# 32 bytes of room behind each k-tile of the weights' high and low parts in a decoder layer

## The chip, the cores and the metric

The kernel runs on one core of a Trainium2 chip. The metric is the device time of one execution in microseconds (us); of the kernel before, three runs have a median of 1816.47 us (1816.28 to 1816.69). Everything is float32 in memory. The tensor engine (PE) takes two operands from the on-chip memory (SBUF, 128 partitions): the stationary one, which a separate instruction (LDWEIGHTS, row PEld) puts into the array, and the moving one, which is streamed past it, one column after the other.

## The reference

One decoder layer, 256 positions wide 2048: a modulation vector from `c` (`w_ada`), a normed input, one large projection, three token mixers side by side, their projections, gates and an output projection, then a gated MLP with a short convolution. Cut to the products with large weights, where the kernel spends its time:

```python
mod = silu(c) @ w_ada + b_ada                      # 2048 x 12288
h = rmsnorm(x, g_mix) * (1 + sc1) + sh1
z = h @ w_in                                       # 2048 x 16392
merged = sig(gm) * (out_m @ w_branch[0]) + sig(gd) * (out_d @ w_branch[1]) + sig(gs) * (out_s @ w_branch[2])
x = x + gt1 * (merged @ w_out)                     # 2048 x 2048
hid = (rmsnorm(x, g_ffn) * (1 + sc2) + sh2) @ w_up # 2048 x 11264
x = x + gt2 * ((silu(conv(hid[:, :5632])) * hid[:, 5632:]) @ w_down)
```

## The kernel before

Each product with a weight matrix runs through `gemm` (line 332). It walks over k-tiles (128 rows of the weight matrix), four at a time. `weights` (line 312) loads four k-tiles by 512 columns (1 MB, line 319) into a tile `raw`, and for each pair of k-tiles makes two tiles of 128 x 2 x 512: `hi`, a rounded copy in the engine's reduced float32 form (ScalarE, ACT, line 324), and `lo`, what the rounding left over (VectorE, DVE, line 326). The activations are kept in a high and a low part as well (`hh` and `hl`, and so on). A product is the sum of three: high by high, high weights by low activations, low weights by high activations.

`mms` (line 346) has three forms, which are told apart by their lines in the profile:

- "F" (line 371): the weights are stationary, 128 columns at a time; 256 columns of activations move. `hi` meets the high and the low activations, `lo` the high ones.
- "T" (line 369): the activations are stationary; the weights move, 512 columns (440 in one part of the input projection).
- "H" (line 355, the up projection): the weights are stationary; with `hi`, the high and low activations of one k-tile move in one matmul of 512 columns, with `lo` the high ones, 256 columns.

Every matmul has its own weight load, for the stationary operand changes each time. In "F" with 512 weight columns and 16 k-tiles, a call issues 16 x 4 x 3 = 192 matmuls; a branch projection (8 k-tiles) issues 96.

Where the operands lie follows from the order of the tile pools and the sizes of their tiles. The pools are laid out one after the other: `const` (small constants, among them `ones_r` and `tri`), `slots` (the activations), `rawp`, `adap`, `hip` (four `hi` buffers), `lop` (four `lo` buffers), `tmp`. In `slots` the slot of tag `s2` is laid out first and has (2 x 4 x 257 + 8) x 4 = 8256 bytes in each partition (line 64), 64 more than a multiple of 512; every other slot has 8192 or 16384, `raw` has 8192, `acc` 2048, `ada` 4096, and `hi` and `lo` have 2 x 512 x 4 = 4096. So in the built program each of the eight weight buffers, each k-tile in it and each activation tile begins at 480 bytes past a multiple of 512; a step of 128 columns is 512 bytes. One GEMM operand is not there: `oml` (line 787), the low part of the first branch's activations, lies in the slot `s2` and begins 64 bytes earlier, at 416. The constants `ones_r` and `tri` begin at 128 past a multiple of 512.

`tri_f` (line 96) is a 128 x 128 mask that is written by GpSimd (line 91) and read once, by the copy to `tri` on line 98. `small` (line 76) is a group of three rotating buffers of 1 KB.

Order: a scheduler sets the order of the instructions on each engine when the program is built; DMA loads are issued by SyncE in the order of the text, tied to one another by `issue_after`.

Of the kernel before, what the change touches and what calls it, by code (L numbers as in the profile page):

```python
# [10 lines left out]
F32 = mybir.dt.float32  # L11
F32R = mybir.dt.float32r
# [5 lines left out]
P = 128  # L18
# [10 lines left out]
EPS = 1e-6  # L29
LAM_INIT = 0.8 - 0.6 * math.exp(-0.3 * 0)  # L30
BIG = 3.0e38

C_MQ, C_MK, C_MV, C_MO = 0, 1024, 2048, 3072
C_IF = 4096
# [5 lines left out]
def kernel(  # L40
# [11 lines left out]
    const = ctx.enter_context(tc.tile_pool(name="const", bufs=1))  # L52
# [3 lines left out]
    hip = ctx.enter_context(tc.tile_pool(name="hip", bufs=4))  # L56
    lop = ctx.enter_context(tc.tile_pool(name="lop", bufs=4))
# [18 lines left out]
    def small(name):  # L76
        return tmp.tile([P, 256], F32, tag="small", name=name, bufs=3)
# [9 lines left out]
    A.copy(ones_r, ones)  # L87

    def masked(name, base, fill, chan, step, cmp):
        m = const.tile([P, P], F32, name=name)  # L90
        nc.gpsimd.memset(m, base)
        nc.gpsimd.affine_select(out=m, in_=m, compare_op=cmp, fill=fill, base=0,
                                pattern=[[step, P]], channel_multiplier=chan)
        return m

    tri_f = masked("tri_f", 1.0, 0.0, 1, -1, ALU.is_gt)
    tri = const.tile([P, P], F32R, name="tri")
    A.copy(tri, tri_f)
    mstrict = masked("mstrict", 1.0, 0.0, -1, 1, ALU.is_gt)
    mcausal = masked("mcausal", 1.0, 0.0, -1, 1, ALU.is_ge)  # L100
    mdiff = masked("mdiff", BIG, -BIG, 1, -1, ALU.is_ge)
    eps_c = const.tile([P, 1], F32, name="eps_c")
# [209 lines left out]
    def weights(rows, nk, n, hold=None):  # L312
        if nk == 2:
            raw = adap.tile([P, 2, 512], F32, tag="ada", name="raw2")
        else:
            raw = rawp.tile([P, 4, 512], F32, tag="raw", name="raw")
        with tc.issue_after(state["load"].ins) if not state["started"] else nullcontext():
            state["started"] = True
            state["load"] = nc.sync.dma_start(raw[:, :nk, :n], rows.rearrange("(k p) f -> p k f", p=P))
        his, los = [], []  # L320
        for k0 in range(0, nk, 2):
            hi = hip.tile([P, 2, 512], F32R, tag="hi", name="hi")
            lo = lop.tile([P, 2, 512], F32R, tag="lo", name="lo")
            A.copy(hi[:, :, :n], raw[:, k0:k0 + 2, :n])  # L324
            with tc.issue_after(hold.ins) if hold else nullcontext():
                state["split"] = V.tensor_tensor(lo[:, :, :n], raw[:, k0:k0 + 2, :n], hi[:, :, :n].bitcast(F32),  # L326
                                                 ALU.subtract)
            his.append(hi)
            los.append(lo)
        return his, los  # L330

    def gemm(orient, act, W, row0, col0, n, kt0, kt1, hold=None, hold_all=False, acc=None):
# [40 lines left out]
        for s0 in range(kt0, kt1, 4):  # L373
            nk = min(4, kt1 - s0)
            r0 = row0 + s0 * P
            wh, wl = weights(W[r0:r0 + nk * P, col0:col0 + n], nk, n, hold if s0 > kt0 or hold_all else None)
            last = s0 + nk >= kt1
            for ks in ([range(nk)] if last else [range(k0, k0 + 2) for k0 in range(0, nk, 2)]):
                for t in range(nt):
                    mms(t, ks, s0, wh, wl)  # L380
            if not last:
                tick()
# [561 lines left out]
    for k in range(0, KD, 2):  # L944
# [3 lines left out]
        for j in range(2):  # L948
            b = b2[:, k + j:k + j + 1]
            hi, lo = h2act(k + j)[:, 0:S], h2act(k + j)[:, S:2 * S]  # L950
# [85 lines left out]
```

## Time and profile before

| | |
|---|---|
| median of three runs | 1816.47 us |
| profiled execution, its own time | 1817.8 us |
| its span, first to last instruction | 1816.1 us |
| mean granted share of PE's clock | 0.994 |
| PE busy / weight loads busy | 1774.3 / 1605.4 us |
| DVE busy / ACT busy | 1333.4 / 907.1 us |
| matmuls | 11045 |

A matmul's duration in the profile is longer than the distance to the next one, since they overlap; a row that says "PE gp L371 x432" in the chain of waits gives a stretch in which nothing but such matmuls follow one another, and its length by its count is the spacing. In operand names, `gp<-hh,hi` is the output tile, then the two inputs; the lines tell which of them moves.

### The profile page before, as it was taken

To read this page: it belongs to the slowest core of one execution; us is meant where nothing else is said; L and a number is where in the kernel's file an instruction comes from. 1 tells how busy PE (TensorE), PEld (TensorE's weight loads), DVE (VectorE), ACT (ScalarE), POOL (GpSimd) and SP (SyncE) were. 2 spreads that over 40 slices of the span, in tenths; PEclk is the share of its full clock that TensorE was granted. 3 is DMA by queue.
4 is the path that set the end of the run, shared out by engine and by line. 5 is a ranking of instruction groups with operands and counts; after the bars stand their busy time and mean duration, and the time that the engine had idled before them with its cause. 6 is when DMAs were issued, how large, how long until landed. Compare 5 with 4: busy or idle time off the path is not lost.

```text
span 1816.1 us, 27533 instructions
## 1 busy us (share of the span) xinstructions
PE 1774.3 (98%) x11045; PEld 1605.4 (88%) x11045; DVE 1333.4 (73%) x1787; ACT 907.1 (50%) x1221; POOL 9.5 (1%) x30
## 2 busy tenths in 40 slices
PE   4989999999999999999999999999999999999998
PEld 4888999999988999999999878888888888888887
DVE  5998867887888687686897568888875556666654
ACT  5533345666565554543444465555553335555532
POOL 0000000000000000000000000000000000000000
PEclk9989999999999999999999999999999999999999
DMA  9988965766778467677898547777765555555563
GB/s 300 338 299 295 315 199 165 262 233 212 240 251 276 163 218 257 219 239 268 286 316 279 184 152 248 254 263 273 263 207 191 197 192 186 188 189 192 196 209 116
DMA packets 219644, 423.55 MB, mean 233 GB/s; under 512 B 8768, under 2 KB 31613, under 8 KB 219005
## 3 DMA queue, kind: packets, MB, share of 16 engines
q1 hardware_dynamic: 217693, 417.56, 68.5%
q0 software_dynamic: 544, 2.11, 0.3%
q8 instruction: 86, 1.41, 0.3%
q10 hardware_dynamic: 1280, 2.14, 0.3%
q14 instruction: 41, 0.34, 0.1%
HBM read 419.68 MB, written 2.10 MB: 232 GB/s over the span
## 4 chain that ended last, share of the span: by engine, by line
PE 91%; DVE 3%; DMA 3%; ACT 1%; issue 1%; SPq 0%; DVEq 0%; ACTq 0%
PE gp L369 30%; PE gp L371 29%; PE acch L355 27%; PE kept L371 2%; DMA raw<-in_w_in_dram 2%; DMA raw<-in_w_ada_dram 1%; DVE lo L326 1%; DVE quads L212 1%; PE psc L627 0%; ACT hi L324 0%; PE pm L228 0%; PE pr L303 0%; DVE acc L212 0%; PE px L935 0%; PE ptf L685 0%
## 5 line engine op out<-in xcount | busy, mean ns | idle before, releaser
L326 DVE TENSOR_TENSOR lo<-raw,hi 128x1024 fp32r<-128x1024 f32 (+1 forms) x608 | 728.1, 1207 | 364.4 <-ACT hi L324 338.1
L324 ACT CAST hi<-raw 128x1024 fp32r<-128x1024 f32 (+1 forms) x608 | 622.7, 1038 | 706.5 <-PE gp L369 225.5
L355 PE MATMUL acch<-h,hi 128*128 128x512 f32 x1408 | 427.9, 395 | 1.8 <-DVE h L952 1.8
L371 PE MATMUL gp<-hh,hi 128*128 128x256 f32 x1152 | 299.8, 285 | 2.3 <-ACT skT L499 2.2
L355 PEld LDWEIGHTS acch<-h,lo 128*128 128x128 f32 x1408 | 252.5, 188 | 54.1
L371 PE MATMUL gp<-hl,hi 128*128 128x256 f32 x1152 | 298.3, 283 | 0.0
L355 PE MATMUL acch<-h,lo 128*128 128x256 f32 x1408 | 263.7, 279 | 0.0
L355 PEld LDWEIGHTS acch<-h,hi 128*128 128x128 f32 x1408 | 221.6, 189 | 10.6 <-DVE h L952 2.0
L371 PEld LDWEIGHTS gp<-hh,hi 128*128 128x128 f32 x1152 | 220.9, 192 | 4.0 <-ACT skT L499 2.4
L371 PEld LDWEIGHTS gp<-hl,hi 128*128 128x128 f32 x1152 | 220.9, 192 | 0.2
L371 PE MATMUL gp<-hh,lo 128*128 128x256 f32 x1152 | 218.3, 284 | 0.5 <-DVE lo L326 0.5
L212 DVE SCALAR_TENSOR_TENSOR acc<-araw,ccol,acc 128x512 f32<-128x512 f32 x240 | 178.8, 745 | 4.0 <-DMA araw<-in_w_ada_dram 2.1
L371 PEld LDWEIGHTS gp<-hh,lo 128*128 128x128 f32 x1152 | 173.2, 192 | 1.1 <-DVE lo L326 0.7
L369 PE MATMUL gp<-hi,hh 128*128 128x440 f32 (+1 forms) x416 | 159.9, 384 | 3.6 <-DVE sv L501 1.4
L369 PE MATMUL gp<-hi,hl 128*128 128x440 f32 (+1 forms) x416 | 158.1, 380 | 0.0
L369 PE MATMUL gp<-hi,ath 128*128 128x512 f32 x352 | 137.0, 389 | 0.0
L369 PE MATMUL gp<-hi,atl 128*128 128x512 f32 x352 | 136.9, 389 | 0.0
L369 PE MATMUL gp<-lo,hh 128*128 128x440 f32 (+1 forms) x416 | 112.9, 378 | 2.3 <-DVE lo L326 2.3
L369 PE MATMUL gp<-lo,ath 128*128 128x512 f32 x352 | 105.8, 389 | 0.0
L369 PEld LDWEIGHTS gp<-hi,hh 128*128 128x128 f32 x416 | 79.3, 191 | 15.8 <-PE gp L369 2.4
L369 PEld LDWEIGHTS gp<-lo,hh 128*128 128x128 f32 x416 | 78.0, 189 | 13.7 <-DVE lo L326 3.6
L369 PEld LDWEIGHTS gp<-hi,hl 128*128 128x128 f32 x416 | 79.3, 191 | 10.4 <-issue 0.7
(346 smaller groups left out, 2059.9 us busy)
## 6 DMA issues: line engine op xcount, KB each, us to landing
raw<-in_w_in_dram SPq DMA_DIRECT2D x98, 1024.0 KB, 5.0
raw<-in_w_up_dram SPq DMA_DIRECT2D x88, 1024.0 KB, 5.1
araw<-in_w_ada_dram SPq DMA_DIRECT2D x128, 512.0 KB, 5.4
raw<-in_w_down_dram SPq DMA_DIRECT2D x44, 1024.0 KB, 5.1
raw<-in_w_ada_dram SPq DMA_DIRECT2D x62, 512.0 KB, 5.2
raw<-in_w_branch_dram SPq DMA_DIRECT2D x24, 1024.0 KB, 5.3
raw<-in_w_in_dram SPq DMA_DIRECT2D x21, 880.0 KB, 4.7
raw<-in_w_out_dram SPq DMA_DIRECT2D x16, 1024.0 KB, 5.2
```

Source lines behind the costliest of these rows:

```text
L212: V.scalar_tensor_tensor(acc, raw[:, k, :], ccol[:, kt:kt + 1], acc, ALU.mult, ALU.add)
L324: A.copy(hi[:, :, :n], raw[:, k0:k0 + 2, :n])
L326: state["split"] = V.tensor_tensor(lo[:, :, :n], raw[:, k0:k0 + 2, :n], hi[:, :, :n].bitcast(F32), ALU.subtract)
L355: T.matmul(acc[t][:, 0:m], lhsT=w[k // 2][:, k % 2, sl], rhs=ah(s0 + k)[:, 0:m], start=start, stop=s0 + k == kt1 - 1 and w is wl, skip_gro ...
L369: T.matmul(o, lhsT=a(s0 + k)[:, sl], rhs=wk[:, :n], **kw)
L371: T.matmul(o, lhsT=wk[:, sl], rhs=a(s0 + k), **kw)
```

## The change

Each `hi` and `lo` tile becomes 128 x 2 x 520, of which the first 512 columns of each k-tile are used. A buffer has 4160 bytes instead of 4096, and the second k-tile in it begins 2080 bytes after the first instead of 2048. The sixteen k-tiles of the eight buffers begin at 0, 32, 64, ..., 480 bytes past the place of the activations, counted modulo 512, each of these once. The copy and the subtraction that fill a buffer with 512 columns now work on two pieces of 512 elements in a partition instead of one of 1024 (the ones with 440 columns were in two pieces before). To make room, `tri_f` is no longer a tile of its own but takes one of the rotating `small` buffers. All tiles from the slots to `adap` lie 512 bytes lower. No instruction is added, taken out or moved: on each engine the same operations stand in the same order.

```diff
+SKEW = 8
...
     def masked(name, base, fill, chan, step, cmp):
-        m = const.tile([P, P], F32, name=name)
+        m = small("tri_f")[:, 0:P] if name == "tri_f" else const.tile([P, P], F32, name=name)
...
-            hi = hip.tile([P, 2, 512], F32R, tag="hi", name="hi")
-            lo = lop.tile([P, 2, 512], F32R, tag="lo", name="lo")
+            hi = hip.tile([P, 2, 512 + SKEW], F32R, tag="hi", name="hi")
+            lo = lop.tile([P, 2, 512 + SKEW], F32R, tag="lo", name="lo")
```

## Rows read from the trace of the kernel before

**Rows 1.** page, part 1: busy us (share of the span) xinstructions

```profile
PE 1774.3 (98%) x11045; PEld 1605.4 (88%) x11045; DVE 1333.4 (73%) x1787; ACT 907.1 (50%) x1221; POOL 9.5 (1%) x30
```

**Rows 2.** page, part 4: the chain that ended last, shares of the span

```profile
PE 91%; DVE 3%; DMA 3%; ACT 1%; issue 1%; SPq 0%; DVEq 0%; ACTq 0%
```

**Rows 3.** chain of waits in order of time: start us, us, what

```profile
291.99 14.40 PE gp L369 x72
...
785.63 51.84 PE gp L371 x432
...
913.30 34.35 PE gp L371 x288
...
948.12 34.35 PE gp L371 x288
...
1185.34 55.84 PE acch L355 x320
...
1349.35 129.88 PE gp L369 x573
```

**Rows 4.** PE groups by form, xcount | busy us, mean ns of one | idle

```profile
L355 PE MATMUL acch<-h,hi 128*128 128x512 f32 x1408 | 427.9, 395 | 1.8 <-DVE h L952 1.8
...
L371 PE MATMUL gp<-hh,hi 128*128 128x256 f32 x1152 | 299.8, 285 | 2.3 <-ACT skT L499 2.2
...
L369 PE MATMUL gp<-hi,ath 128*128 128x512 f32 x352 | 137.0, 389 | 0.0
...
L369 PE MATMUL gp<-hi,hh 128*128 128x440 f32 x224 | 83.9, 375 | 2.8 <-DVE sv L501 1.1 <-DVE dk L501 1.0 <-DVE dv L501 0.7
...
L369 PE MATMUL gp<-hi,hh 128*128 128x512 f32 x192 | 76.0, 396 | 0.8 <-ACT skT L499 0.5 <-DVE sv L501 0.3
```

**Rows 5.** instructions of one tile, GEMM lines: duration ns min/median/max

```profile
L371 PE MATMUL gp<-oml,hi x128: 277/279/286, 866.7 to 981.7; 128*128 128x256 f32 x128
...
L371 PE MATMUL gp<-odh,hi x128: 280/283/468, 715.7 to 842.8; 128*128 128x256 f32 x128
...
L369 PE MATMUL gp<-hi,atl x352: 389/389/397, 1348.5 to 1810.1; 128*128 128x512 f32 x176
...
L355 PE MATMUL acch<-h,hi x1408: 387/396/497, 1078.5 to 1701.7; 128*128 128x512 f32 x176
...
L355 PE MATMUL acch<-h,lo x1408: 274/278/285, 1079.8 to 1702.3; 128*128 128x256 f32 x176
```

**Rows 6.** instructions of four lines with a constant as stationary: duration ns min/median/max

```profile
L303 PE MATMUL pr<-parts,ones_r x16: 393/395/398, 883.6 to 1349.0; 128*128 128x512 f32 x16
...
L567 PE MATMUL puA<-hlB,ones_r x4: 282/290/297, 309.3 to 388.2; 128*128 128x256 f32 x4
...
L568 PE MATMUL puA<-hlB,ones_r x4: 281/282/286, 309.4 to 388.3; 128*128 128x256 f32 x4
...
L565 PE MATMUL puB<-hlB,tri x4: 278/281/281, 306.5 to 385.8; 128*128 128x256 f32 x4
```

**Rows 7.** DVE and ACT groups by form of the split, same columns as rows 4

```profile
L326 DVE TENSOR_TENSOR lo<-raw,hi 128x1024 fp32r<-128x1024 f32 x552 | 669.0, 1221 | 349.9 <-ACT hi L324 327.8 <-PE gp L369 17.0 <-PE pdt L612 1.7
...
L326 DVE TENSOR_TENSOR lo<-raw,hi 128x880 fp32r<-128x880 f32 x56 | 59.2, 1068 | 14.5 <-ACT hi L324 10.3 <-PE gp L369 3.2 <-ACT ht L432 0.8
...
L324 ACT CAST hi<-raw 128x1024 fp32r<-128x1024 f32 x552 | 572.0, 1050 | 636.4 <-PE gp L369 201.4 <-PE gp L371 173.8 <-PE acch L355 157.8
...
L324 ACT CAST hi<-raw 128x880 fp32r<-128x880 f32 x56 | 50.7, 926 | 70.1 <-DMA raw<-in_w_in_dram 41.0 <-PE gp L369 24.0 <-DVE ez L570 4.0
```

**Rows 8.** PE waits for the low part: us in total, times, longest us

```profile
PE gp L369 <- DVE lo L326: 2.3, 2, 1.3
...
PE gp L371 <- DVE lo L326: 0.5, 1, 0.5
```

**Rows 9.** lines 98 and 429: duration ns min/median/max, first and last start us

```profile
L98 ACT CAST tri<-tri_f x1: 292/292/292, 2.8 to 2.8; 128x128 fp32r<-128x128 f32 x1
...
L429 DVE TENSOR_SCALAR ht<-xnT,a,b x2: 408/410/411, 28.6 to 29.0; 128x256 f32<-128x256 f32 x2
```

## Prediction

> **What bounds the kernel now.** I read the page's busy shares first. The tensor engine is busy 98% of the span with 11045 matmuls, VectorE 73%, ScalarE 50% [rows 1]. The chain that ended last gives PE 91% and VectorE 3% [rows 2], so the question is what one matmul costs. The chain in order of time has long stretches of nothing but matmuls of one form; length by count is their spacing [rows 3]: 51.84 us by 432 is 120.0 ns for form F (256 columns), 129.88 by 573 is 226.7 ns for T with 512 columns, 14.40 by 72 is 200.0 ns for T with 440, 55.84 by 320 is 174.5 ns as the mean of H, which alternates 512 and 256 columns. A spacing of exactly 120.0 ns over 432 matmuls while loads, copies and subtractions go on beside them says that it is made inside the engine and not by a neighbour.
>
> Two stretches of F differ. The rows at 913.30 and 948.12 hold 288 matmuls each, 192 of the gate and 96 of the first branch, in 34.35 us. With 192 at 120.0 ns (23.04 us) the 96 are left 11.31 us, or 117.8 ns. Shape, order and engine are the same; what differs is that one in three of the 96 moves `oml`, the only GEMM operand that does not begin at 480 bytes modulo 512 but 64 lower. The durations say it too: 279 ns median for `oml`, 283 for `odh` [rows 5]. So the place of one operand against the other does change the spacing. Durations exceed spacings by a constant 162 to 163 ns (283 against 120.0, 389 against 226.7), so a row of durations can be read as a row of spacings.
>
> The Trainium skill (TensorE: Matmul & The Clock Gate, Step-by-step: what each phase is for) says that the weight load and the moving operand have independent read ports and that loading the next weights takes no bandwidth from the running matmul. The 117.8 against 120.0 ns do not fit it, if the place is the cause; by the rule alone the change would be worth 0 us.
>
> **The change part by part.** Nothing is added or moved on any engine, so the terms are differences of spacing times counts.
>
> F: 128 x 3 groups for `kept`, 1152 x 3 for `hh`/`hl` (one of them in [rows 4]) and 128 x 9 for the three branches make 4992 matmuls; 384 of them, those of the first branch, already have the mixed distance, which leaves 4608. In the changed kernel the stationary buffers lie at sixteen distances from the activations. The nearest row is the 117.8 ns, a gain of 2.2 ns; but there one operand in three is shifted, by one fixed amount. The few other matmuls whose own or next weights lie elsewhere are on both sides of 283: 278/281/281 with `tri`, 281/282/286 and 282/290/297 with `ones_r` [rows 6]. I take half the gain: 4608 x -1.1 = -5.1 us. Ends: the shortest 256-column matmul is 274 ns in H [rows 5], 9 under 283, -41 us; the median of 290 is 7 over, +32 us.
>
> T with 512 columns: three groups each of 352, 192 and 128, one of each of the first two sizes in [rows 4], are 2016. Here the moving operand is the one that is spread out. With all distances equal its duration is 389 and hardly leaves it (389/389/397 [rows 5]), near the lowest 512-column value anywhere, 387 in H. The only 512-column matmuls with another distance, line 303, take 393/395/398 [rows 6], and H, whose mix of widths never settles, has a median of 396. T repeats one good state because every step is like the last; with the distance changing at each k-tile I expect it to leave it. I take 394, between the lowest and the median of line 303: +5 ns x 2016 = +10.1 us. Ends: 387, -4 us; 398, +18 us.
>
> T with 440 columns: three groups of 224 [rows 4] are 672. No row shows another distance; I take 0, with T's ends scaled by the count: -1 to +6 us.
>
> H: 1408 x 2 [rows 4]. It already wanders, 387 to 396 and 274 to 278 from least to median [rows 5], although all distances are multiples of 512, so other distances add one more reason to wander: 0. Ends: both widths at their shortest, (9 + 4)/2 = 6.5 ns x 2816 = -18 us; upward the 256-column maximum is 7 over its median, and with half of that for both widths, 4 ns, +11 us.
>
> The split: 552 subtractions and 552 copies now work on two pieces. Those with 440 columns always did: 1068 ns for 880 elements against 1221 for 1024 is 1.06 ns for each of the 144 more, and 926 against 1050 is 0.86 [rows 7]. If the second piece costs c and an element s, then c = 144 s - 153 on VectorE and 144 s - 124 on ScalarE; s is at most 1221/1024 = 1.19 and 1050/1024 = 1.03, so c is at most 19 and 24 ns, and at the slopes themselves it is 0. I take 0. At the upper end VectorE would work 552 x 19 = 10 us longer, ScalarE 13; but PE waits 2.8 us in all for `lo` [rows 8], and the two engines are idle 27% and 50% of the span, which hides it. Without that cover it would cost the 10.
>
> `tri_f`: read on ScalarE at 2.8 us; the buffers of its new group are first written again at 28.6 [rows 9]. 0. The loads go to places 512 bytes lower: 0.
>
> Sum on the profiled execution: 1817.8 - 5.1 + 10.1 = 1822.8 us. That execution is 1.3 above the median of the runs, so 1821.5.
>
> The same page (Back-to-back issue gap) puts the spacing of a matmul by itself at its columns over 2.4 GHz and 2.5 ns: 109 ns for 256 columns, 216 for 512. As an estimate from that page, all forms at this spacing would save about 120 us, 1697 us. The trace has no stretch of F, T or H at it.
>
> **The rivals.** 1. F gains as much as the first branch shows and T keeps 389: 4608 x -2.2 = -10.1 us, 1806.4, faster. For it: 117.8 is the only steady row of a shifted operand. Against it: line 303. It decides from the point at which F's gain passes 0.44 of T's loss per matmul (2016/4608).
> 2. The reads of the two operands hardly meet any more: F at 278, the least of `tri` (-5 x 4608 = -23), T at 387 (-4), H halfway to its shortest (-9): -36 us, 1780. For it: 274 and 387 exist. Against it: they exist at equal distances too, so distance alone isn't what makes them.
> 3. Nothing happens: the first branch is faster for another reason, and the distance is not felt. 1816.5. For it: the steady 120.0 and 226.7 hold for distances of 0, 512, 1024 and 1536 alike. That is also what the page's rule on the ports gives.
> 4. F is disturbed for the worse too: F at 286, the longest of line 568 (+3, +14 us), T at 398 (+18): +32 us, 1848.
>
> **How the numbers follow.** Forecast 0.38, its own range 1816 to 1829 (F between -2.2 and 0, T between +3 and +7); rival 1 0.22, rival 2 0.10, rival 3 0.14, rival 4 0.16. A change of 0.2% (3.6 us) is about what a measurement of this kernel can tell from none. Faster: rival 1 (0.20 of it), rival 2, and 0.03 each of the forecast and rival 3, 0.36. Within 0.2%: 0.10 of rival 3, 0.08 of the forecast, 0.02 of rival 1, 0.20. Slower: 0.27 of the forecast, rival 4, and 0.01 of rival 3, 0.44. The range, 1800 to 1840, leaves out rival 2 and the upper half of rival 4.
>
> **What would show it.** Length by count in the chain's long rows: F below 120.0 (119 by my sum), T at 512 columns up to about 232 with a median duration of 394 and a wider span of durations, H still at 174 to 175. The subtraction and the copy still at 1221 and 1050 ns. PE's waits for `lo` still a few us. I am wrong about T if its durations stay at 389 and wrong about F if they stay at 283; if both stay, rival 3 holds. If the first branch's stretch of 96 does not differ from the gates' any more, the sixteen distances have replaced its one.

## The result and the profile after

The changed kernel takes 1821.44 us (median of 8 runs, 1817.85 to 1823.81) against 1816.55 us before (8 runs): a ratio of 1.0024, 95% interval 1.0012 to 1.0035, so 2 to 6 us slower. Its profiled span is 1819.6 us against 1816.1; part of the difference between the medians can be the clock, of which the granted share was 0.994 in the profiled execution before and 0.993 in this one. 1821.5 was predicted.

Page, part 1, of the changed kernel (busy us, share of the span, xinstructions). All lines of its profile are one higher than before, because of the added constant.

```profile
PE 1779.2 (98%) x11045; PEld 1602.4 (88%) x11045; DVE 1334.5 (73%) x1787; ACT 906.0 (50%) x1221; POOL 9.5 (1%) x30
```

PE has the same 11045 matmuls and is busy 4.9 us longer; nothing else moves by more than 1.1 [rows 1], apart from the weight loads, which are shorter by 3. So the answer is in the matmuls' spacing. The clock does not make it: in the stretches of 432 and of 573 below, and in the same two of the kernel before, the granted share is 1.00. The chain of waits of the changed kernel in order of time (start us, us, what), the stretches that answer to [rows 3]:

```profile
291.61 14.38 PE gp L370 x72
...
782.93 51.12 PE gp L372 x432
...
909.26 34.06 PE gp L372 x288
...
943.78 34.06 PE gp L372 x288
...
1182.60 55.99 PE acch L356 x320
...
1347.08 132.70 PE gp L370 x573
```

Length by count gives spacings. F (line 372): 51.12 / 432 = 118.3 ns, it was 120.0. T with 512 columns (line 370): 132.70 / 573 = 231.6, it was 226.7. T with 440: 14.38 / 72 = 199.7, it was 200.0. H (line 356): 55.99 / 320 = 175.0, it was 174.5. In the stretches of 288, 192 gate matmuls at 118.3 leave 34.06 - 22.72 = 11.34 us for the 96 of the first branch, 118.1 ns each: they no longer differ from the gates.

The durations say the same. Single tiles of the changed kernel (duration ns min/median/max):

```profile
L372 PE MATMUL gp<-oml,hi x128: 277/281/286, 862.9 to 977.1; 128*128 128x256 f32 x128
...
L372 PE MATMUL gp<-odh,hi x128: 274/281/472, 713.7 to 839.3; 128*128 128x256 f32 x128
...
L370 PE MATMUL gp<-hi,atl x352: 387/393/399, 1346.2 to 1813.5; 128*128 128x512 f32 x176
```

`odh` went from a median of 283 to 281 and now begins at 274; `atl`, which hardly left 389 [rows 5], spreads from 387 to 399 around 393. The groups by form of the changed kernel (xcount | busy us, mean ns | idle), one per form and the two of the split:

```profile
L327 DVE TENSOR_TENSOR lo<-raw,hi 128x1024 fp32r<-128x1024 f32 x552 | 669.5, 1222 | 353.7 <-ACT hi L325 330.3 <-PE gp L370 17.7 <-PE pdt L613 1.6
L325 ACT CAST hi<-raw 128x1024 fp32r<-128x1024 f32 x552 | 570.8, 1048 | 643.0 <-PE gp L370 210.8 <-PE gp L372 167.5 <-PE acch L356 160.4
L356 PE MATMUL acch<-h,hi 128*128 128x512 f32 x1408 | 427.0, 394 | 1.8 <-DVE h L953 1.8
L372 PE MATMUL gp<-hh,hi 128*128 128x256 f32 x1152 | 297.9, 284 | 2.5 <-ACT skT L500 2.3 <-ACT hi L325 0.2
...
L370 PE MATMUL gp<-hi,ath 128*128 128x512 f32 x352 | 138.7, 394 | 0.0
...
L370 PE MATMUL gp<-hi,hh 128*128 128x512 f32 x192 | 76.7, 399 | 0.3 <-DVE sv L502 0.3
```

The splits in two pieces cost what those in one piece did, 1222 and 1048 ns against 1221 and 1050 [rows 7]. PE's waits for the low part (us in total, times, longest) are as short as in [rows 8]:

```profile
PE gp L370 <- DVE lo L327: 2.0, 2, 1.1
...
PE gp L372 <- DVE lo L327: 0.5, 1, 0.5
```

What is to be settled is why F gains and T loses. In what follows, "distance" is how many bytes the weights begin after the activations within a partition. Theory A: the spacing depends on where the operands lie against each other. Rivals: B, the change of distance from step to step does it, not the distance; C, the splits in two pieces do; D, the move of `tri_f`, and of everything after it, by 512 bytes does; E, the place of the weights by itself does.

### The profile page after: what moved, and what is told of

It reads as the page before. It is cut to its first block, busy times and chain, and to the rows that moved or that the text cites. A ratio compares the mean times of both kernels' runs of the same rounds, so it can differ in the third digit from the quotient of the medians.

```text
span 1819.6 us, 27533 instructions
## 1 busy us (share of the span) xinstructions
PE 1779.2 (98%) x11045; PEld 1602.4 (88%) x11045; DVE 1334.5 (73%) x1787; ACT 906.0 (50%) x1221; POOL 9.5 (1%) x30
## 4 chain that ended last, share of the span: by engine, by line
PE 92%; DVE 4%; DMA 2%; issue 1%; ACT 0%; SPq 0%; DVEq 0%; ACTq 0%
PE gp L370 30%; PE gp L372 29%; PE acch L356 27%; PE kept L372 2%; DMA raw<-in_w_ada_dram 2%; DVE quads L213 1%; DVE lo L327 1%; DMA raw<-in_w_in_dram 1%; DVE acc L213 0%; PE psc L628 0%; ACT hi L325 0%; PE pm L229 0%; PE pr L304 0%; PE ptf L686 0%; PE pm L219 0%
## 5 line engine op out<-in xcount | busy, mean ns | idle before, releaser
L325 ACT CAST hi<-raw 128x1024 fp32r<-128x1024 f32 (+1 forms) x608 | 621.5, 1036 | 711.3 <-PE gp L370 232.1
```

## The experiments

### Distances held constant, matmuls alone

Three streams of matmuls in the layer's forms and nearly its orders, at sixteen distances, and once with the changed kernel's gaps:

```
def place(d, stride=512):
    return lambda kt, c, n: wts[:, 2 * d + kt * stride + c:2 * d + kt * stride + c + n]
...
for i in range(16):
    f, t, h = stream(place(4 * i))     # F, T, H sections, 32 * i bytes
...
f, t, h = stream(place(0, 520))        # Fz, Tz, Hz
```

> This kernel leaves the layer out (its output is a copy of x) and only streams matmuls in the layer's three forms: F (weights' k-tile as lhsT, activations 256 wide moving), T (activations as lhsT, weights 512 wide moving), H (weights as lhsT, activations 512 wide for the high part, 256 for the low). Nothing is split or loaded beside them. Sections Fa to Fp, Ta to Tp and Ha to Hp hold the weights at one constant distance from the activations, 0, 32, 64 ... 480 bytes beyond a multiple of 512; Fz, Tz and Hz have the changed kernel's 32 bytes after each k-tile, so the distance changes from step to step. Theory A (the spacing of two matmuls depends on where, within 512 bytes, the moving operand lies against the weights loaded next): the sixteen constant sections differ from one another by 2 ns or more per matmul; Fa is 120.0 ns and Ta 226.7 ns as in the kernel before, Fz about 118.4 and Tz about 231.6 as in the changed one, near the mean of the sixteen. Rival B (it is the change of distance from step to step, not the distance): all sixteen F at 120.0, all sixteen T at 226.7, and only Fz and Tz at 118.4 and 231.6. Rival C (the two-piece splits on ScalarE and VectorE disturb TensorE, or their timing does): with no split here Fz equals Fa and Tz equals Ta within 0.3 ns.

It ran once, at a granted clock of 1.0, as did the other two kernels of matmuls alone. The chain of this kernel in order of time; the letters i, k, p are 256, 320 and 480 bytes, c is 64:

```profile
79.94 11.31 PE Fc L48 x96
91.25 11.01 PE Tc L48 x48
...
282.19 11.51 PE Fi L48 x96
293.70 10.91 PE Ti L48 x48
...
349.54 11.31 PE Fk L48 x96
360.85 11.01 PE Tk L48 x48
...
518.28 11.20 PE Fp L48 x96
529.48 11.21 PE Tp L48 x48
...
551.79 11.36 PE Fz L48 x96
563.15 11.15 PE Tz L48 x48
```

Fc and Fk, Tc and Tk agree to 0.01 us: from 256 bytes on the values repeat (the first section, with the engine's start in it, aside). The second eight letters, length by count in ns:

| distance modulo 256 | F | T, 512 columns | H |
|---|---|---|---|
| 0 | 119.9 | 227.3 | 174.1 |
| 32 | 118.3 | 233.3 | 175.6 |
| 64 | 117.8 | 229.4 | 173.6 |
| 96 | 120.1 | 233.3 | 175.9 |
| 128 | 118.6 | 232.1 | 174.4 |
| 160 | 119.9 | 234.2 | 176.6 |
| 192 | 117.7 | 233.3 | 173.1 |
| 224 | 116.7 | 233.5 | 173.4 |
| gaps of 32 (z) | 118.3 | 232.3 | 175.2 |

(A section's first steps are in these numbers, which puts T some 0.5 ns high.) This accounts for both changes. At distance 0, where all GEMM operands of the kernel before but `oml` lie, F has one of its worst values and T its best. A kernel that runs through all distances gets about the mean of the column, F 118.6 and T 232.1. With no split in it, this kernel gives Fz and Tz nearly the changed kernel's 118.3 and 231.6. Rival B falls, since the constant distances differ from one another, and so does C for the spacings, since no split runs here.

### Only `tri_f` moved

```diff
-        m = const.tile([P, P], F32, name=name)
+        m = small("tri_f")[:, 0:P] if name == "tri_f" else const.tile([P, P], F32, name=name)
```

> The kernel before, with only tri_f moved out of the constants, as the change does to make room; no room behind the k-tiles, so every tile from tri on lies 512 bytes lower and all distances within 512 bytes are as before. Theory A and rivals B and C all expect the time of the kernel before (ratio 1.000 within 0.001), F at 120.0 ns and T at 226.7. Rival D (the move by 512 bytes, or tri_f's new place, is what made the difference): the changed kernel's ratio of 1.0024 shows here, with F at 118.4 and T at 231.6 ns.

Ratio 0.9997 (0.9983 to 1.0010), and the two stretches of the chain have the lengths of before:

```profile
785.86 51.84 PE gp L371 x432
...
1350.61 129.88 PE gp L369 x573
```

Rival D is out: the 512 bytes change neither spacing.

### High and low activations moved apart, and all operands together

```
for i in range(8):
    for j in range(8):
        f, t, u = stream(8 * i, 8 * j, 0)      # high, low activations, weights
        ...
for i in range(8):
    f, t, u = stream(8 * i, 8 * i, 8 * i)      # X and Y
    ...
```

> Like the first kernel of distances, this one leaves the layer out and only streams matmuls, here with the weights fixed and the high and low activations moved by 0, 32 ... 224 bytes each, independently (second and third letter of a section's name, a to h). F and T as before, U is T with 440 wide moving weights. In sections Xa to Xh (form F) and Ya to Yh (form T) weights and activations are moved together by 0 to 224 bytes, so that their distance stays 0. Theory A, as the first kernel left it (the distance modulo 256 bytes sets the spacing): Faa 120.0 and Taa 226.7 ns; with both activations 32 bytes up (Fbb, Tbb), a distance of 224, 116.7 and 233.2; Fcc 117.8, Fhh 118.3, Tgg 228.9; all eight X at 120.0 and all eight Y at 226.7. Rival E (what counts is the place of the weights by itself, not the distance): all 64 F alike at 120.0, and Xb to Xh with the values that the first kernel showed for its letters b to h (118.3, 117.8, 120.0, 118.7, 120.0, 117.8, 116.7). Open for both: U at distance 0 is 200.0 ns as in the layer; elsewhere by the neighbouring form T up to 6 ns more; and unequal letters give values between 113 and 122 (F) and 226 and 238 (T).

The second and third letter of a section give the place of the high and of the low activations, from a (0) to h (224 bytes); U is T with 440 columns. Where the activations are moved up, the distance is 256 less that. The chain of this kernel in order of time:

```profile
206.05 11.31 PE Fag L45 x96
...
302.25 11.20 PE Fbb L45 x96
...
591.09 10.88 PE Fcc L45 x96
...
1457.30 11.39 PE Fff L45 x96
...
1757.18 10.99 PE Tgg L45 x48
...
2089.48 11.51 PE Xb L45 x96
2100.98 10.91 PE Yb L45 x48
...
2224.00 11.51 PE Xh L45 x96
2235.51 10.92 PE Yh L45 x48
```

Fbb at 11.20 / 96 = 116.7 ns and Tgg at 10.99 / 48 = 229.0 are as expected. All eight X last 11.51 or 11.52 us and all eight Y 10.91 or 10.92, the times of distance 0 in the table: weights and activations moved together leave the spacing as it was, so rival E falls for these streams. The 56 sections with unequal letters lie inside the bounds that were written, F from 115.9 to 119.9 and T from 229.0 to 234.2; U is at 200.0 to 203.3 in all sections read. One of them is the first branch of the kernel before: Fag, with the high activations at 0 and the low ones 64 bytes below a multiple of 256, as `omh` and `oml` lie, has 11.31 / 96 = 117.8 ns, the value that [rows 3] left for that branch. So the place of `oml` alone is enough to make it. Some values were missed: Fcc, 192 bytes, has 10.88 / 96 = 113.3 ns where the table has 117.7, Fgg, 64 bytes, lasts 10.90 us, 113.5, and Fff, 96 bytes, has 118.6 where the table has 120.1. The same distance gave two spacings.

### All weights at one distance: 64 bytes, 224 bytes

In the layer, with `tri_f` moved and the split in one piece; for 224 bytes the tile has 56 columns instead of 16:

```diff
+    roomp = ctx.enter_context(tc.tile_pool(name="roomp", bufs=1))
+    room = roomp.tile([P, 16], F32, name="room")
     hip = ctx.enter_context(tc.tile_pool(name="hip", bufs=4))
```

> The kernel before with tri_f moved and 64 bytes of room ahead of the first hi buffer, none behind the k-tiles: all hi and lo buffers lie at one distance of 64 bytes (modulo 512) from the activations, and the splits stay in one piece. Theory A: the spacings that the first kernel of distances showed at 64 bytes: F 117.8 ns instead of 119.9 (4224 x -2.1 = -9.0 us), T with 512 wide 228.9 instead of 227.1 (2016 x +1.8 = +3.6), H 173.4 instead of 174.5 (2816 x -1.1 = -3.0), form T with 440 wide unknown (672 x 0 to 6 = 0 to 4): about 1808 us, 1806 to 1813, faster than both kernels. Rival B (only a changing distance does anything): F 120.0, T 226.7, 1816.5 us.

> As with 64 bytes, but 224 bytes of room ahead of the first hi buffer. Theory A: F 116.7 ns instead of 119.9 (4224 x -3.3 = -13.8 us), the largest gain that a distance gave in form F, T with 512 wide 233.2 instead of 227.1 (2016 x +6.1 = +12.3 us), H 173.5 instead of 174.5 (2816 x -1.0 = -2.8), T with 440 wide unknown (0 to +4): about 1812 to 1816 us; the two terms of opposite sign of the prediction, both larger, nearly cancel. Rival B: F 120.0, T 226.7, 1816.5 us, the spacings tell it apart where the time does not.

The chain at 64 bytes:

```profile
369.25 12.84 PE gp L373 x109
...
772.83 48.98 PE gp L373 x432
...
1164.51 55.49 PE acch L357 x320
...
1327.52 131.16 PE gp L371 x573
```

and at 224:

```profile
777.58 50.41 PE gp L373 x432
...
1341.26 133.69 PE gp L371 x573
```

With 224 bytes the kernel takes 1815.31 us, ratio 0.9997 (0.9988 to 1.0006): F at 50.41 / 432 = 116.7, T at 133.69 / 573 = 233.3, both as the first experiment had them, the two cancelling. No distance changes from step to step here, and both forms have left 120.0 and 226.7: rival B is out in the layer too. With 64 bytes it takes 1796.24 us, ratio 0.9889 (0.9874 to 0.9904), faster than both kernels, and 12 us below what I expected. T at 131.16 / 573 = 228.9 and H at 55.49 / 320 = 173.4 came as written; F came at 48.98 / 432 = 113.4 instead of 117.8. Over the whole layer F's groups fall by 5 ns, as this one of the groups by form at 64 bytes does, from 285 [rows 4] to 280:

```profile
L373 PE MATMUL gp<-hh,hi 128*128 128x256 f32 x1152 | 290.7, 280 | 2.9 <-ACT skT L501 2.1 <-ACT hi L326 0.8
```

4608 x -5 = -23 us, 2016 x +2.2 = +4.4 for T and 2816 x -1.1 = -3.1 for H are -22; the span is 21.0 us shorter, 1795.1. The size of F's term was off, by the second spacing that the grid had shown. (The two expectations also count 4224 matmuls of form F where 4608 are at distance 0, which is 0.8 us at 64 bytes and 1.3 at 224.) Both spacings occur in this one kernel, on the same tiles `hh` and `hl`: the stretch of 109 has 12.84 / 109 = 117.8.

### One distance, different starts

The grid had shown 113.3 ns too, at distances for which the first experiment had 117.8. A last kernel of matmuls puts one short matmul ahead of each section:

```
for name, d in (("F", 0), ("G", 16), ("J", 48)):     # 0, 64, 192 bytes
    ...
    for i in range(16):
        lead = [(16 * (i + 1), f[0][1], acts[:, 0:16 * (i + 1)])]
        section(name + LETTERS[i], lead + f + f + f)
```

> Again only matmuls (the layer is left out), all in form F: sections Fa to Fp at distance 0, Ga to Gp at 64 bytes, Ja to Jp at 192 bytes, 144 matmuls each, and ahead of each section one matmul with 16 (a), 32 (b) ... 256 (p) moving columns, so that the streams begin at different moments against what went before. The kernels so far gave two spacings at 64 and 192 bytes: 117.8 ns in the first kernel of distances, 113.3 in the second, and a mixture in the layer. Theory F (a stream settles into a repeating cycle; at some distances there are several, and the start chooses): F at 120.0 after every lead, G and J at 113.3 after some leads and 117.8 after others, each constant through its section. Rival G (something other than the start told the two kernels apart, such as the absolute places or the neighbouring sections): all 16 G alike and all 16 J alike.

Its chain in order of time:

```profile
256.04 17.38 PE Fo L45 x145
...
307.89 17.07 PE Gb L45 x145
324.96 16.45 PE Gc L45 x145
...
576.65 17.07 PE Jb L45 x145
```

At 64 bytes seven of the sixteen sections have the length of Gc, 16.43 to 16.46 us, and nine that of Gb, 17.07 to 17.08; nothing lies between. The difference, 0.62 us over 144 matmuls, is 4.3 ns, that of 117.8 and 113.4. At distance 0 the sections from Fc to Fp all last 17.38 to 17.40. At 192 all sixteen leads give 17.07 to 17.09, though the grid has 113.3 there: theory F holds for 64 bytes; for 192 it is not shown, and what told the two kernels apart there stays open. So at 64 bytes either of two spacings can hold for a whole section. The sixteen sections read the same tiles with the same matmuls but for the lead (the output alternates between two buffers, and the seven fast sections, c, f, g, i, l, m and n, fall on both), so what decides is how the stream begins: the lead, or the state in which the section ahead of it ended, which these runs do not separate. The layer's F at 64 bytes is near the faster spacing in its longest stretch and at the slower one in the stretch of 109.

### The buffers' distances without the gap between k-tiles

```diff
-            hi = hip.tile([P, 2, 512], F32R, tag="hi", name="hi")
+            hi = hip.tile([P, 1024 + 16], F32R, tag="hi", name="hi")[:, 0:1024].rearrange("p (k f) -> p k f", k=2)
```

and the same for `lo`; this is the difference to the kernel before, and `tri_f` is moved here too.

> The changed kernel's buffers without the gap between their two k-tiles: the 64 bytes of room lie behind the second k-tile, so hi and lo buffers keep the sixteen-distance kernel's buffer addresses (0, 64, 128, 192 bytes modulo 256 from the activations, twice), both k-tiles of a buffer have its distance, and every split is one contiguous piece as in the kernel before. Theory A (distance modulo 256): spacings near the mean over these four distances in the kernels that held them constant, F 117 +- 2 instead of 119.9 (-13 to -4 us), T with 512 wide 230.3 instead of 227.1 (+6.5), H within 1 ns of before: 1810 to 1819 us, T certainly above 229. Rival C (the split in two pieces is what disturbs TensorE): with one-piece splits F is back at 120.0, T at 226.7 and the time at 1816.5 us.

1811.23 us, ratio 0.9974 (0.9962 to 0.9986). The chain:

```profile
776.22 50.59 PE gp L371 x432
...
1339.08 132.40 PE gp L369 x573
```

F is at 117.1 and T at 231.1 with splits in one piece, so rival C is out in the layer as well: T is lost with them too. The distances here are 0, 64, 128 and 192; with 113.3 ns at 64 and 192 the table's mean over them is 116.3, with its own values 118.5, and F lies between. It gains more than in the changed kernel: 4608 x (117.1 - 118.3) = -5.5 us, and 2016 x (231.1 - 231.6) = -1.0 for T; together with H (55.70 / 320 = 174.1, -0.9 ns x 2816 = -2.5 us) -9 us, where the spans differ by 9.8. (The terms are rough: the first stretch of H, 608 matmuls, is 0.8 us longer here than in the changed kernel.) The same kind of change, with other numbers in it, is faster than the kernel before.

### The activations moved instead of the weights

`hh` and `hl` are moved by 192 bytes, which puts the weights at 64 from them; the room behind them makes 256 in all, so that all other tiles keep their distances. `tri_f` is moved here too.

```diff
...
+    slots.tile([P, 48], F32, tag="room", name="room")
     hh = slots.tile([P, KD, S], F32R, tag="hh", name="hh")
     hl = slots.tile([P, KD, S], F32R, tag="hl", name="hl")
+    slots.tile([P, 16], F32, tag="room2", name="room2")
```

> The weights' buffers stay as in the kernel before (no room behind k-tiles, distance 0 from the slots); instead the two large activation tiles hh and hl (and h2, which takes their place for the up projection) lie 192 bytes higher than a multiple of 256, which makes the weights' distance from them 64 bytes, as in the kernel with 64 bytes ahead of all weights. The down and out projections' activations (ath, atl, mgh, mgl) and the branches' stay at distance 0. Theory A: F on hh and hl (3840 of 4608 outside the om branch) 114 to 115 ns as with 64 bytes for all, the rest of F 120.0; T with 512 wide on ath and mgh back at 226.7, on hh 229; H 173.4 as there: 3840 x -5.4 = -20.7, 576 x +1.9 = +1.1, 2816 x -1.1 = -3.1: about 1794 us, 1792 to 1800. Rival E (the place of the weights by itself): nothing moves, 1816.5 us, F at 120.0.

1795.01 us, ratio 0.9884 (0.9866 to 0.9902): with the kernel at 64 bytes for all, the fastest of this case. The chain:

```profile
551.32 33.89 PE gp L369 x148
...
770.68 49.93 PE gp L371 x432
...
927.49 33.09 PE gp L371 x288
...
1164.39 55.48 PE acch L355 x320
...
1327.37 129.90 PE gp L369 x573
```

T on `ath` and `atl`, at distance 0 again, is back at 129.90 / 573 = 226.7; on `hh` and `hl` it is at 33.89 / 148 = 229.0. In the stretch of 288, 96 matmuls of the first branch at 117.8 [rows 3] leave 33.09 - 11.31 = 21.78 us for 192 gate matmuls on `hh` and `hl`: 113.4 ns. The stretch of 432 is one of gates (288) and a branch that stayed at 0 (144): 288 x 113.4 + 144 x 120.0 = 49.94 us, as measured. H is at 173.4. Where the operand was moved the spacing changed, and where it was not it stayed, in one and the same kernel: rival E is out.

## Why the prediction was right, point by point

- **F**, -1.1 ns expected, -1.7 measured (120.0 to 118.3): 4608 x -1.7 = -7.8 us instead of -5.1. The value was half of the 2.2 ns that the first branch's shifted operand showed, and no row stood behind the half; the reading of that stretch, 117.8 ns against 120.0, was the right clue, as Fag bears out.
- **T with 512 columns**, +5 ns expected, +4.9 measured in the long stretch (226.7 to 231.6); by the groups' means it is +5 on `ath` (389 to 394) and +3 on `hh` (396 to 399), so 2016 x 4 to 5 = +8 to +10 us instead of +10.1. The rows of line 303 [rows 6] gave the size. They show one distance only: `ones_r` is at 128 and the moving `parts`, a tile of `adap`, at 480, so 352 bytes, or 96 modulo 256, where the table has 233.3 ns for T, near the mean of the eight, 232.1. That this one could stand for sixteen was luck.
- **T with 440 columns**: 0 expected, 200.0 to 199.7.
- **H**: 0 expected, +0.5 ns x 2816 = +1.4 us. The means over the groups agree that little moved: 395 to 394 with `hi`, 279 to 280 with `lo`.
- **The first branch's advantage** went, as written: 118.1 against the gates' 118.3.
- **Split, `tri_f`**: 0 expected and found.

The sum is about +2 to +4 us; the profiled span grew by 3.5, the medians by 4.9 (2 to 6 by the interval), +5.0 was predicted. The terms are off by 3 us or less each, F and T downward and H upward, so the sum holds better by the medians than by the stretches. That it meets the median to 0.1 us is luck; the way in which F and T went is not.

One reason was wrong though its number held. I argued that T repeats one good state because every step is like the last, and would leave it because the distance changes at each k-tile. At a constant 224 bytes every step is like the last too, and T runs at 233.3. T lost because 0 is its best distance: every other one in the table is worse, and so is a mixture of them. By the same table F gained because 0 is one of its worst.

Of the rivals, the third (nothing is felt) falls with every experiment that changes a distance: F of one shape has 113.4, 116.7, 118.3 or 120.0 ns in the long stretches of the layer as its operands are placed. The Trainium skill (TensorE: Matmul & The Clock Gate, Step-by-step: what each phase is for) says that loading the next weights takes no read bandwidth from the running matmul; by that alone these would be equal. The runs show that the place matters, not that a read port is shared. By the formula of the Trainium skill (the same page, Back-to-back issue gap) for a matmul by itself, the estimate for 256 columns is 109 ns; no stretch reached it, and 113.3 came nearest. The first rival, F faster while T keeps its place, is not what this change does, but it nearly exists: in the kernel with the moved activations, at 1795 us, the T of `ath` and `atl` keeps 226.7. The second rival's -5 ns for F is reached too, at 64 bytes, but there T is 2 ns worse and H, at 173.4, is 1.1 ns shorter instead of 3.

Open: which two operands of neighbouring matmuls have to be at the distance (the running one's moving operand and the next one's weights, or its own), and what in the memory repeats every 256 bytes. No run here separates them. In F a block of `hi` stays stationary for two matmuls in a row, with the high and then with the low activations, and each still has its own load (11045 loads for 11045 matmuls); "the stationary operand changes each time", in the section on the kernel before, holds for T and H alone.

## What to carry to other kernels

When PE is the bound and its spacing in a long stretch is steady but above that of another stretch of the same shape, compare the addresses of their operands modulo 256 bytes; moving one group of tiles was worth 1.1% here. Find the distance for each form of matmul by itself, in a kernel that holds it constant, check it in the kernel that is to gain (at 64 bytes the two differed by 4.4 ns), and move only the operands of the forms that gain: a spread over all distances gives every form the mean, which takes from the form that lay best. And read the spacing as length by count in the chain of waits, where 2 ns in 120 are seen at once, while PE's busy share stays at 98%; look at the granted clock of the stretch first.

## What the runs showed of the hardware

- The spacing of float32r matmuls, each with its own weight load, depends on the distance of the operands modulo 256 bytes: F 113.3 to 120.1 ns, T with 512 columns 226.7 to 234.2, H 173.1 to 176.6. Moving both operands together changed nothing (11.51 or 11.52 us at all eight places for F, 10.91 or 10.92 for T).
- T with 440 columns hardly takes part: the stretch of 72 has 14.38 to 14.41 us in every version of the layer, 200 ns each, and the highest value read in the grid, with the high and low activations at different places, is 203.3.
- At one and the same distance (64 bytes) F can hold either of two spacings, 117.8 or 113.3 ns, through a section of 144 matmuls, and how the stream begins chooses.
- Differences of 1 or 2 us between two runs of this layer can be the clock. Of the 12 runs with only `tri_f` moved, the four at a granted share of 0.991 or 0.992 took 1817.95 to 1821.92 us, the eight at 0.994 to 0.997 took 1812.34 to 1816.67. The first stretch of H (608 matmuls) lasted 105.73 us with all weights at 64 bytes and 108.12 at 224: the granted share of its first 10 us was 1.00 and 0.78, the latter with part of them at 1.2 instead of 2.4 GHz, after the same short pauses of PE.
